# The last block of an encoder step: squares moved to ScalarE, whole-pass weight buffers, one table load, output pieces in free weight tiles on two store queues

## The chip, the cores and the metric

One core of one Trainium2 chip runs the whole program. Its engines are TensorE (PE; its weight loads are listed as PEld), VectorE (DVE), ScalarE (ACT), GpSimd (POOL) and SyncE (SP), which issues transfers. The metric is the device time of one execution in microseconds, the median over several runs. Lower is better.

## The reference, cut to what matters

The program computes one layer of a streaming encoder for 512 prompt frames, 16 meta tokens and 64 sample frames in float32: attention, then a feed-forward network, then a final RMSNorm. Only the end matters here:

```python
x = x + (jax.nn.silu(h @ lp['ffn_w_gate']) * (h @ lp['ffn_w_up'])) @ lp['ffn_w_down']
...
y_prompt = rmsnorm(xp[:, N_META:], final_norm_g)
y_sample = rmsnorm(xs, final_norm_g)

def rmsnorm(x, g):
    y = xf * lax.rsqrt(jnp.mean(xf * xf, axis=-1, keepdims=True) + EPS)
    return y * g
```

D_MODEL is 2048 and D_FF 5632. 576 tokens go through the feed-forward network (512 prompt and 64 sample tokens).

## The kernel before

**Layout.** Activations are kept transposed: a chunk of 128 model features lies on the partitions, the 576 tokens along the free dimension, in two halves `h` of 288 (`QH`). There are 16 such chunks, `y[0]` to `y[15]`. Float32 products are made of three products in a rounded format: `split(hi, lo, src)` rounds a tile to `hi` on ScalarE (L156) and takes the remainder `lo = src - hi` on VectorE (L153). `mm3` (L185 to L189) then adds `hi*hi`, `hi*lo` and `lo*hi` on TensorE.

**The down projection.** The 44 chunks of the hidden dimension come as 22 pairs and are taken in six blocks of 4, 4, 4, 4, 4 and 2 pairs. In the first five blocks `down_rows` uses a seven-product scheme (L1207 and L1211). The last block, of two pairs, uses plain products: `plain_rows`, called for each token half `h` (0, then 1) and each of eight pairs `d` of output chunks. One such call is called a pass here. It has 24 matmuls: two output chunks `f`, four weight chunks `k`, three products. For each `f`, it splits a 128x512 piece of weights into a `wh` and a `wl` tile, of which there are two buffers each. The raw weights of a pass (512 KB) come from HBM through two buffers of the tile `raw` in the pool `fd`; `fetch_raw` issues the load of a later pass on SyncE's queue behind each pass.

**The end of a pass.** VectorE adds the product to `y` (L1462). `squares` then squares the chunk half on GpSimd (L1485, L1488), adds the square to a running sum `sqs[h]` (L1489), and ScalarE multiplies the chunk in place by the gain of the final norm (L1490). ScalarE's scaling overwrites what GpSimd squares, so it waits for it.

**The output.** `finish(h, ahead)` is a generator. It turns `ahead` groups first: a group is four 128x128 transposes on TensorE into one bank of PSUM (L1503), for a set of four chunks `q` and a token group `j` (three token groups in each half, of 64, 128 and 96 or 128, 128 and 32 tokens). Then it sums the squares over the partitions with a matmul against ones for each token group (L1515, L1517), and takes the reciprocal root with a logarithm and an exponential on ScalarE and three small steps on VectorE (`rsqrt`, L165 to L169). Then, for each of twelve groups, it scales the turned rows by that root into an output piece `ot` of up to 128x512 (odd pieces on ScalarE, L1526, even ones on VectorE, L1528) and stores the piece from SyncE's queue (L140). The pieces lie in two buffers of a tag `ws` and one of a tag `ot`. The first half's `finish` is run in between the second half's passes, two steps behind each pass from the second on. The second half's runs behind the last pass.

**The order.** Tiles, buffers and semaphores are placed by a scheduler that simulates the program; within this part of the kernel it may issue an engine's instructions in another order than they are written, when their data allows. ScalarE's function tables are loaded by an instruction of its own (ACT_TABLE_LOAD), which the compiler puts ahead of a function that is not in the loaded set. The program preloads a set with logarithm and exponential once, at L134. The gate's Silu (L1364) loads another.

Of the kernel before, what the change touches and what calls it, by code (L numbers as in the profile page):

```python
# [11 lines left out]
F32 = mybir.dt.float32  # L12
F32R = mybir.dt.float32r
AF = mybir.ActivationFunctionType
ALU = mybir.AluOpType
# [4 lines left out]
P = 128  # L20
D = 2048
KC = D // P
SEQ, NM, NS, PAST = 512, 16, 64, 128
# [5 lines left out]
QH = TQ // 2  # L29
# [86 lines left out]
def encoder_step(  # L116
# [8 lines left out]
    V, S, G = nc.vector, nc.scalar, nc.gpsimd  # L125
    st = Streams()
    PE = OrderedTensorEngine(tc, st)
# [11 lines left out]
    def store(dst, src):  # L139
        nc.sync.dma_start(dst, src)  # L140
# [8 lines left out]
    def f32(ap):  # L149
        return ap.bitcast(F32)  # L150

    def sub_lo(lo, src, hi):
        V.tensor_tensor(lo, src, f32(hi), op=ALU.subtract)  # L153

    def split(hi, lo, src):
        S.activation(hi, src, AF.Copy)  # L156
        sub_lo(lo, src, hi)
# [27 lines left out]
    def mm3(outs, wh, wl, xh, xl, start, stop):  # L185
        n = len(outs)
        for p, (w, x) in enumerate(((wh, xh), (wh, xl), (wl, xh))):
            for i in range(n):
                PE.matmul(outs[i], w, x[i], start=start and p == 0, stop=stop and p == 2)  # L189
# [117 lines left out]
    with ExitStack() as ph:  # L307
# [29 lines left out]
        ones = f32(ones_r)  # L337
# [5 lines left out]
        with tc.tile_pool(name="xn", bufs=1, reuse_waits="tile") as xn:  # L343
# [41 lines left out]
            raw, both = {}, {}  # L385
# [702 lines left out]
    PE = nc.tensor  # L1088
    wp_cm.__exit__(None, None, None)
    def pool(name, side="left"):  # L1090
        cm = tc.tile_pool(name=name, bufs=1, side=side, reuse_waits="tile")
        return cm.__enter__(), lambda: cm.__exit__(None, None, None)
# [133 lines left out]
    ws = {}  # L1226
# [13 lines left out]
    for i in range(KC):  # L1240
# [3 lines left out]
        for hf in range(2):  # L1244
            wh, wl = ws.pop(2 * i + hf)
# [24 lines left out]
    fw, close_fw = pool("fw")  # L1270

    def load_pair(pool, src, c0, first=0):
        r = pool.tile([P, 16, 256], F32, name="raw", tag="raw", bufs=1)
        for i in range(2 - first):
            r0 = (first + i) * 1024
            load(r[:, 8 * i:8 * i + 8], src[r0:r0 + 1024, c0:c0 + 256].rearrange("(k p) c -> p k c", p=P))
        return r

    raw = load_pair(fr, w_gate, 0, 1)
# [8 lines left out]
    def squad(dtype=F32):  # L1288
        return fr.tile([P, 4, QH], dtype, name="s", tag="s", bufs=1)
# [37 lines left out]
    def builder(m0, count, plain, by_product=False):  # L1327

        places = {1: 0, 2: 1, 4: 2, 5: 3} if plain else {1: 0, 2: 2, 3: 3, 5: 4, 6: 5, 4: 6, 7: 7}
        todo = [(m, p) for m in range(m0, m0 + count) for p in places]  # L1330
        if by_product:
            order = [p for p, _ in CHAIN]
            todo.sort(key=lambda mp: order.index(mp[1]))
        for m, p in todo:
            hl = bc.tile([P, 2, QH], F32R, name=f"b{p}_{m % 8}")
            load(f32(hl), opspill[m, :, places[p]])
            operands[m % 8, p] = hl[:, 0], hl[:, 1]
            yield
# [47 lines left out]
    start = builder(0, blocks[0], False, True)  # L1386
    for u in range(FC // 2):
        out = {}
        for which, wsrc in (("g", w_gate), ("u", w_up)):
            first = turn == 0  # L1390
            now = raw[:, 0:8] if first else raw
            if turn < FC - 1:
                raw = load_pair((fr, fb)[(turn + 1) % 2], (w_up, w_gate)[turn % 2], (turn + 1) // 2 * 256)
            turn += 1
            c = fc.tile([P, 2, TQ], F32, name="c", tag="c" + which, bufs=1 + (which == "g"))
            chain = () if first else CHAIN if u == FC // 2 - 1 and which == "u" else WIDE
            take = combined(*quarters(c[:, 0, :], c[:, 1, :]), chain)
            if u == FC // 2 - 1 and which == "u":
                raw = fr.tile([P, 16, 256], F32, name="raw", tag="raw", bufs=1)
# [25 lines left out]
        g, w = out["g"], out["u"]  # L1425
# [4 lines left out]
        parts = [(0, w.rearrange("p f (h c) -> p (f h) c", h=2))]  # L1430
        if u < FC // 2 - blocks[-1]:
            b11, b12, b21, b22 = quarters(w[:, 0, :], w[:, 1, :])
            t = g.rearrange("p f (h c) -> p (f h) c", h=2)
# [9 lines left out]
    fd, close_fd = pool("fd")  # L1443

    def plain_rows(m0, n, d, hs, slots, done):

        banks = {(f, h): pmt()[:, 0:QH] for f in range(2) for h in hs}
        r = fetched.pop((m0, d, hs))
        for g in range(0, n, 2):
            for f in range(2):  # L1450
                wh = fw.tile([P, 4, P], F32R, name="wh", tag="wh", bufs=2)
                wl = fw.tile([P, 4, P], F32R, name="wl", tag="wl", bufs=2)
                split(wh, wl, r[:, 2 * g:2 * g + 4, f * P:(f + 1) * P])
                for k in range(4):
                    m = slots[g + k // 2]
                    ops = [operands[m, ((1, 2), (4, 5))[k % 2][h]] for h in hs]
                    mm3([banks[f, h] for h in hs], wh[:, k, :], wl[:, k, :], [o[0] for o in ops],
                        [o[1] for o in ops], g + k == 0, g + k == n + 1)
        for f in range(2):
            for h in hs:  # L1460
                c = y[2 * d + f][:, h * QH:(h + 1) * QH]
                V.tensor_tensor(c, c, banks[f, h], op=ALU.add)  # L1462
                done(2 * d + f, h)
# [12 lines left out]

    tok = [[(0, NS), (NS, P), (192, 96)], [(QH, P), (416, P), (544, 32)]]
    sqs = {}
    s4 = squad()

    def squares(i, h):
        c = y[i][:, h * QH:(h + 1) * QH]
        if i == 0:
            sqs[h] = s4[:, h]
            G.tensor_tensor(sqs[h], c, c, op=ALU.mult)  # L1485
        else:
            t = s4[:, 2 + i % 2]
            G.tensor_tensor(t, c, c, op=ALU.mult)  # L1488
            G.tensor_tensor(sqs[h], sqs[h], t, op=ALU.add)  # L1489
        S.activation(c, c, AF.Copy, scale=gE[:, i:i + 1])  # L1490

    def finish(h, ahead):

        groups = [(q, j) for q in range(4) for j in range(3)]

        def turned(q, j):
            o, n = tok[h][j]  # L1500
            ps = pmt()
            for k in range(4):
                PE.transpose(ps[0:n, k * P:(k + 1) * P], y[q * 4 + k][:, o:o + n], ident)  # L1503
            return ps

        held = []
        for g in groups[:ahead]:
            held.append(turned(*g))
            yield
        pc = pmt()  # L1510
        vc = yy.tile([P, 3], F32, name=f"vc{h}")
        rc = yy.tile([P, 3], F32, name=f"rc{h}")
        V.memset(vc, 1.0)
        for j, (o, n) in enumerate(tok[h]):
            PE.matmul(pc[0:n, 2 * j:2 * j + 2], sqs[h][:, o - h * QH:o - h * QH + n], ones[:, 0:2],  # L1515
                      start=True, stop=True)
            V.tensor_scalar(vc[0:n, j:j + 1], pc[0:n, 2 * j:2 * j + 1], 1.0 / D, EPS, op0=ALU.mult, op1=ALU.add)  # L1517
        rsqrt(rc, vc)
        yield
        for i, (q, j) in enumerate(groups):  # L1520
            o, n = tok[h][j]
            ps = held.pop(0) if held else turned(q, j)
            tag, bufs = ("ws", 2) if i % 3 < 2 else ("ot", 1)
            ot = yy.tile([P, 4, P], F32, name="ot", tag=tag, bufs=bufs).rearrange("p a b -> p (a b)")
            if i % 2:
                S.activation(ot[0:n], ps[0:n, :], AF.Copy, scale=rc[0:n, j:j + 1])  # L1526
            else:
                V.tensor_scalar(ot[0:n], ps[0:n, :], rc[0:n, j:j + 1], None, op0=ALU.mult)  # L1528
            cs = slice(q * 512, (q + 1) * 512)
            if o == 0:  # L1530
                store(y_sample[:, cs], ot[0:NS])
            else:
                store(y_prompt[o - NS:o - NS + n, cs], ot[0:n])
            yield

    wanted, m0 = [], 0
# [16 lines left out]
    for bi, n in enumerate(blocks):  # L1553
        slots = [(first + k) % 8 for k in range(n)]
        if bi + 1 < len(blocks):
            build = builder(first + n, blocks[bi + 1], bi + 2 == len(blocks))

            def step():
                next(spilling, None)
                if bi or d:  # L1560
                    next(build, None)

            for d in range(KC // 2):
                if bi == 0 and d + 1 < KC // 2:
                    load_y(d + 1)
                down_rows(first, n, d, slots, step)
                fetch_raw()
                if bi + d == 0:
                    for _ in spilling:
                        pass  # L1570
                    close_rw()
                    yy, close_yy = pool("yy", "right")
            for _ in build:
                pass
        else:
            before = iter(())
            for h in range(2):
                for d in range(KC // 2):
                    plain_rows(first, n, d, (h,), slots, squares)
                    fetch_raw()  # L1580
                    if d:
                        for _ in range(2):
                            next(before, None)
                before = finish(h, 5 * h)
            for _ in before:
                pass
        first += n
# [74 lines left out]
```

## Time and profile before

| | us |
|---|---|
| median of 3 runs | 2474.02 (2471.19 to 2477.39) |
| the profiled execution | 2474.84 |
| its span, first to last instruction | 2473.1 |
| first matmul of the last block (L189) | at 2386.85 |
| last block's passes end, transposes follow | at 2452.67 |
| first output piece of the second half | at 2459.27 |
| last store issued | at 2470.2 |

| engine | busy us | share of the span |
|---|---|---|
| PE | 2391.3 | 97% |
| DVE | 1856.6 | 75% |
| ACT | 1133.8 | 46% |
| POOL | 817.1 | 33% |

Times in the trace count from the span's first instruction. A row of the timeline has its start, its length in us, the engine, the line, the operation, the tiles as out<-in, and the count of instructions merged in it. In brackets stands the idle time of the engine before it and what ended that. In the rows of waits the numbers are the total in us, the times and the longest. In the rows of groups, busy time in us, mean ns of one, and then the idle time before them with its releasers. In the rows of transfers, KB each and the median us from issue to landing.

### The profile page before, as it was taken

How to read it: one execution, taken by the hardware profiler on the slowest of the kernel's cores; microseconds unless marked ns; L12 is line 12 of the kernel's file. 1: busy time of each engine (PE TensorE's matmuls, PEld its weight loads, DVE VectorE, ACT ScalarE, POOL GpSimd, SP SyncE). 2: the span in 40 equal slices, each digit the busy share in tenths (PEclk: the TensorE clock that was granted, in tenths of full speed). 3: DMA queues.
4: the chain of work that ended last, by engine and by line, in shares of the span. 5: the costliest groups of instructions: out<-in, count | busy, mean ns of one | idle time of the engine just before them, and what ended most of it. 6: DMA issues, size and time to landing. Idle time of an engine off the chain costs nothing. (4 is left out here: it accounts for less than half of the span.)

```text
span 2473.1 us, 44094 instructions
## 1 busy us (share of the span) xinstructions
PE 2391.3 (97%) x17544; PEld 2343.1 (95%) x17544; DVE 1856.6 (75%) x2748; ACT 1133.8 (46%) x1977; POOL 817.1 (33%) x525
## 2 busy tenths in 40 slices
PE   7999999999999999999999999999999999999997
PEld 7999999999998998999999999999999999999986
DVE  5666676666664788778778788787787888888875
ACT  5445545334453554444444444444444333333345
POOL 1100000120000455555555655555554222222245
PEclk9999999999999999999999999999999999999999
DMA  7432233253323644344444444443546873563334
GB/s 223 142 96 83 83 98 94 66 156 102 99 82 118 185 152 146 113 163 151 134 152 141 142 151 134 157 158 113 170 151 212 301 243 125 198 220 108 102 103 145
DMA packets 361972, 353.03 MB, mean 143 GB/s; under 512 B 25087, under 2 KB 319637, under 8 KB 361765
## 3 DMA queue, kind: packets, MB, share of 16 engines
q1 hardware_dynamic: 359535, 343.43, 43.5%
q0 software_dynamic: 1904, 6.24, 0.8%
q8 instruction: 138, 2.26, 0.4%
q10 hardware_dynamic: 325, 0.53, 0.1%
q14 instruction: 70, 0.57, 0.1%
HBM read 271.68 MB, written 81.16 MB: 143 GB/s over the span
## 5 line engine op out<-in xcount | busy, mean ns | idle before, releaser
L1207 PE MATMUL m<-b,wh 128*128 128x288 f32 x7168 | 1050.1, 295 | 16.6 <-DVE y L1472 8.5
L1207 PEld LDWEIGHTS m<-b,wh 128*128 128x128 f32 x7168 | 982.8, 188 | 23.6 <-issue 16.7
L153 DVE TENSOR_TENSOR wl<-raw,wh 128x512 fp32r<-128x512 f32 (+1 forms) x457 | 600.3, 1314 | 59.3 <-ACT wh L156 59.0
L1211 PE MATMUL m<-b,wl 128*128 128x288 f32 x3584 | 583.4, 298 | 11.7 <-DVE wl L153 11.5
L156 ACT ACTIVATE wh<-raw 128x512 fp32r<-128x512 f32 (+1 forms) x457 | 380.1, 832 | 410.3 <-PE m L1207 275.1
L1211 PEld LDWEIGHTS m<-b,wl 128*128 128x128 f32 x3584 | 512.4, 188 | 21.5 <-DVE wl L153 21.5
L1186 POOL TENSOR_TENSOR ws<-raw 128x1024 f32<-128x1024 f32 (+1 forms) x85 | 201.7, 2373 | 619.3 <-DVE wl L153 289.7
L156 ACT ACTIVATE wh<-ws 128x512 fp32r<-128x512 f32 (+1 forms) x170 | 144.2, 848 | 222.3 <-DVE ws L1189 180.0
L108 PE MATMUL ps<-xh,wh 128*128 128x296 f32 x992 | 225.9, 309 | 0.1
L108 PE MATMUL ps<-xl,wh 128*128 128x296 f32 x992 | 217.7, 301 | 0.3 <-DVE xl L161 0.3
L108 PE MATMUL ps<-xh,wl 128*128 128x296 f32 x992 | 216.9, 300 | 0.0
L1195 POOL TENSOR_TENSOR raw<-raw 128x1024 f32<-128x1024 f32 (+1 forms) x85 | 207.1, 2437 | 6.6
L153 DVE TENSOR_TENSOR wl<-ws,wh 128x512 fp32r<-128x512 f32 (+1 forms) x170 | 164.5, 968 | 17.5 <-ACT wh L156 17.4
L1346 DVE TENSOR_TENSOR c<-c,s 128x288 fp32r<-128x288 f32 x168 | 84.6, 533 | 110.6 <-POOL c L1437 59.7
L108 PEld LDWEIGHTS ps<-xh,wh 128*128 128x128 f32 x992 | 161.6, 191 | 3.7 <-issue 0.6
L108 PEld LDWEIGHTS ps<-xl,wh 128*128 128x128 f32 x992 | 162.3, 190 | 1.0 <-DVE xl L161 0.9
L108 PEld LDWEIGHTS ps<-xh,wl 128*128 128x128 f32 x992 | 162.2, 190 | 0.0
L1472 DVE TENSOR_TENSOR y<-y,m 128x288 f32<-128x288 f32 x280 | 126.0, 450 | 46.1 <-PE m L1211 46.1
L153 DVE TENSOR_TENSOR wl<-wr,wh 128x1024 fp32r<-128x1024 f32 (+1 forms) x110 | 120.7, 1097 | 31.7 <-ACT wh L156 30.4
L156 ACT ACTIVATE wh<-wr 128x1024 fp32r<-128x1024 f32 (+1 forms) x110 | 102.2, 929 | 75.3 <-PE ps L108 50.7
L1345 ACT ACTIVATE s<-c 128x288 fp32r<-128x288 f32 x168 | 63.2, 434 | 151.9 <-POOL c L1429 130.6
L1429 POOL TENSOR_TENSOR c<-c 128x576 f32<-128x576 f32 x44 | 101.1, 2297 | 80.6 <-DVE c L1303 78.9
(370 smaller groups left out, 3194.7 us busy)
## 6 DMA issues: line engine op xcount, KB each, us to landing
raw<-in_ffn_w_gate SPq DMA_DIRECT2D x44, 1024.0 KB, 5.5
raw<-in_ffn_w_up SPq DMA_DIRECT2D x44, 1024.0 KB, 7.9
b<-opspill SPq DMA_DIRECT2D x148, 288.0 KB, 5.9
raw<-in_ffn_w_down SPq DMA_DIRECT2D x38, 1024.0 KB, 5.6
wr<-in_w_in SPq DMA_DIRECT2D x56, 512.0 KB, 4.1
opspill<-s SPq DMA_DIRECT2D x42, 576.0 KB, 3.1
opspill<-c SPq DMA_DIRECT2D x42, 576.0 KB, 3.1
wr<-in_w_out SPq DMA_DIRECT2D x16, 512.0 KB, 4.3
```

Of the source, the lines that this page charges most:

```text
L108: self.tc.keep_in_program_order(self.pe.matmul(out, lhsT, rhs, start=start, stop=stop))
L153: V.tensor_tensor(lo, src, f32(hi), op=ALU.subtract)
L156: S.activation(hi, src, AF.Copy)
L1186: G.tensor_tensor(x, y, z, op=ALU.add)
L1195: G.tensor_tensor(y, x, y, op=ALU.subtract)
L1207: PE.matmul(banks[p], wh[:, k, :], x, start=first and new and k == 0 and x is hi, stop=False, skip_group_check=not new)
L1211: PE.matmul(banks[p], wl[:, k, :], hi, start=False, stop=last and k == n - 1, skip_group_check=not new)
L1345: S.activation(hi[:, k], src[:, k], AF.Copy)
L1346: V.tensor_tensor(src[:, k].bitcast(F32R), src[:, k], f32(hi[:, k]), op=ALU.subtract)
L1429: G.tensor_tensor(w[:, f, :], w[:, f, :], g[:, f, :], op=ALU.mult)
L1472: V.tensor_tensor(c, c, banks[p], op=ALU.add)
```

## The change

It has four parts, all in the last block and behind it.

1. `plain_rows`: the tiles `wh` and `wl` hold both output chunks of a pass (twice the size, still two buffers each), so weights can be split up to two passes ahead.
2. `squares`: in the first half the odd chunks are squared by ScalarE in place of GpSimd. In the second half the last two chunks (`LATE = 2`) are squared by ScalarE and not added to the running sum; the matmul against ones takes three parts, the sum and these two squares.
3. A preload of the set with logarithm and exponential, in front of the last block, pinned behind what ScalarE has before it. The first half's `finish` gets one step behind the second pass in place of two.
4. `finish`: in the second half eight of the twelve pieces lie in two tiles of the weights' tag `raw`, four pieces in each. The other four, and all pieces of the first half, lie in the two buffers of `ws`. The pieces 1, 3, 4 and 7 of the second half are stored from GpSimd's queue.

```diff
@@ plain_rows
         for g in range(0, n, 2):
+            wh = fw.tile([P, 2, 4, P], F32R, name="wh", tag="wh", bufs=2)
+            wl = fw.tile([P, 2, 4, P], F32R, name="wl", tag="wl", bufs=2)
             for f in range(2):
-                wh = fw.tile([P, 4, P], F32R, name="wh", tag="wh", bufs=2)
-                wl = fw.tile([P, 4, P], F32R, name="wl", tag="wl", bufs=2)
-                split(wh, wl, r[:, 2 * g:2 * g + 4, f * P:(f + 1) * P])
+                split(wh[:, f], wl[:, f], r[:, 2 * g:2 * g + 4, f * P:(f + 1) * P])
...
-                    mm3([banks[f, h] for h in hs], wh[:, k, :], wl[:, k, :], [o[0] for o in ops],
+                    mm3([banks[f, h] for h in hs], wh[:, f, k], wl[:, f, k], [o[0] for o in ops],
@@ squares
+    LATE = 2
...
-        if i == 0:
+        if h and i >= KC - LATE:
+            sqs[h, i] = s4[:, 2 + i % 2]
+            S.activation(sqs[h, i], c, AF.Square)
+        elif i == 0:
             sqs[h] = s4[:, h]
             G.tensor_tensor(sqs[h], c, c, op=ALU.mult)
         else:
             t = s4[:, 2 + i % 2]
-            G.tensor_tensor(t, c, c, op=ALU.mult)
+            if h or i % 2 == 0:
+                G.tensor_tensor(t, c, c, op=ALU.mult)
+            else:
+                S.activation(t, c, AF.Square)
             G.tensor_tensor(sqs[h], sqs[h], t, op=ALU.add)
@@ finish
-            PE.matmul(pc[0:n, 2 * j:2 * j + 2], sqs[h][:, o - h * QH:o - h * QH + n], ones[:, 0:2],
-                      start=True, stop=True)
+            parts = [sqs[h]] + [sqs[h, i] for i in range(KC - LATE, KC) if h]
+            for q in parts:
+                PE.matmul(pc[0:n, 2 * j:2 * j + 2], q[:, o - h * QH:o - h * QH + n], ones[:, 0:2],
+                          start=q is parts[0], stop=q is parts[-1])
...
-            tag, bufs = ("ws", 2) if i % 3 < 2 else ("ot", 1)
-            ot = yy.tile([P, 4, P], F32, name="ot", tag=tag, bufs=bufs).rearrange("p a b -> p (a b)")
+            k = i - i // 3
+            if h and i % 3 < 2:
+                if k % 4 == 0:
+                    four = fd.tile([P, 4, 512], F32, name="ot", tag="raw", bufs=2)
+                ot = four[:, k % 4]
+            else:
+                ot = yy.tile([P, 4, P], F32, name="ot", tag="ws", bufs=2).rearrange("p a b -> p (a b)")
...
+            out_queue = G.dma_start if h and i in (1, 3, 4, 7) else store
@@ the last block's loop
             before = iter(())
+            tc.keep_in_program_order(S.preload_act_table_set("natural_log_exp_and_others"))
             for h in range(2):
                 for d in range(KC // 2):
                     plain_rows(first, n, d, (h,), slots, squares)
                     fetch_raw()
-                    if d:
-                        for _ in range(2):
-                            next(before, None)
+                    for _ in range(min(d, 2)):
+                        next(before, None)
                 before = finish(h, 5 * h)
```

More of the change, by code (lines that the diff above doesn't have):

```diff
@@ L1529, in finish @@
             cs = slice(q * 512, (q + 1) * 512)
+            out_queue = G.dma_start if h and i in (1, 3, 4, 7) else store
             if o == 0:
-                store(y_sample[:, cs], ot[0:NS])
+                out_queue(y_sample[:, cs], ot[0:NS])
             else:
-                store(y_prompt[o - NS:o - NS + n, cs], ot[0:n])
+                out_queue(y_prompt[o - NS:o - NS + n, cs], ot[0:n])
             yield
```

## The prediction, made before the change was run

> **What bounds the kernel now.** I read the page first for the whole, then the chain of work that ended last, then the last block alone: its waits, its timeline engine by engine, and its groups by form.
>
> ```profile
> span 2473.1 us, 44094 instructions
> PE 2391.3 (97%) x17544; PEld 2343.1 (95%) x17544; DVE 1856.6 (75%) x2748; ACT 1133.8 (46%) x1977; POOL 817.1 (33%) x525
> ...
> by line: DMA out<-ot 6.9%; ACT ot L1526 1.5%; DVE ot L1528 1.5%; issue 1.2%; SPq L140 0.8%; DVE rc L169 0.2%; DVE vc L167 0.2%; DVE vc L168 0.2%; ACTq L1526 0.0%; DVEq L1528 0.0%
> ```
>
> TensorE (PE) is busy 97% of the span, so nearly everything that can be won lies where it idles. The second row is the chain within the window from 2385 to 2473 us: it is made of output pieces, and of their landing above all. So the change, which touches only the last block of rows (from 2386.85 us, the first matmul of L189) and the tail, has two stretches to work on: 66 us of passes, and a tail without matmuls.
>
> The passes. One pass is 24 matmuls for two row chunks of one token half. These rows are one pass in the middle of the first half, first TensorE, then the three engines that feed it.
>
> ```profile
> 2414.15 0.42 PE L189 MATMUL m<-b,wh 128*128 128x288 f32 x2
> ...
> 2416.92 0.43 PE L189 MATMUL m<-b,wh 128*128 128x288 f32 x2
> 2417.76 0.40 PE L189 MATMUL m<-b,wl 128*128 128x288 f32 x1 [0.41 <-DVE wl L153]
> ...
> 2414.48 1.16 POOL L1488 TENSOR_TENSOR s<-y 128x288 f32<-128x288 f32 x1
> ...
> 2418.33 1.17 POOL L1488 TENSOR_TENSOR s<-y 128x288 f32<-128x288 f32 x1
> ...
> 2415.68 0.54 ACT L1490 ACTIVATE y<-y,gT 128x288 f32<-128x288 f32 x1 [1.28 <-POOL s L1488]
> 2416.12 0.62 ACT L156 ACTIVATE wh<-raw 128x512 fp32r<-128x512 f32 x1
> ...
> 2416.77 0.93 DVE L153 TENSOR_TENSOR wl<-raw,wh 128x512 fp32r<-128x512 f32 x1 [0.78 <-ACT wh L156]
> ```
>
> Read it as a chain. GpSimd (POOL) squares a row chunk until 2415.64; the scaling on ScalarE (ACT) waits 1.28 us for that; the weight split of the next half pass stands behind the scaling in ScalarE's order, VectorE (DVE) takes its remainder from 2416.77 to 2417.70, and TensorE goes on at 2417.76 after an idle time. Between 2414.15 and 2416.92 lie seven triples of matmuls, 2.77/7 = 0.396 us each, so a pass of eight triples is worth 3.17 us; the pitch from one pass to the next is 2418.33 - 2414.48 = 3.85 us. About 0.68 us of each pass is lost. GpSimd sets that pitch:
>
> ```profile
> L1489 POOL TENSOR_TENSOR s<-s 128x288 f32<-128x288 f32 x30 | 28.3, 942 | 2.3
> L1488 POOL TENSOR_TENSOR s<-y 128x288 f32<-128x288 f32 x30 | 25.7, 855 | 8.9 <-DVE y L1462 8.7
> ...
> L156 ACT ACTIVATE wh<-raw 128x512 fp32r<-128x512 f32 x31 | 19.1, 619 | 4.6 <-PE m L189 2.3 <-DMA raw<-in_ffn_w_down 1.3 <-DVE wl L153 1.0
> L1490 ACT ACTIVATE y<-y,gT 128x288 f32<-128x288 f32 x32 | 17.1, 535 | 23.3 <-POOL s L1488 22.0 <-POOL s L1485 1.1
> ...
> L153 DVE TENSOR_TENSOR wl<-raw,wh 128x512 fp32r<-128x512 f32 x32 | 26.4, 827 | 11.7 <-ACT wh L156 11.4
> L1462 DVE TENSOR_TENSOR y<-y,m 128x288 f32<-128x288 f32 x32 | 14.4, 449 | 8.7 <-PE m L189 8.7
> ```
>
> Two squares and two adds are 2 x 0.855 + 2 x 0.942 = 3.59 us by the means, more than the 3.17 us that TensorE needs. What all this costs TensorE between 2386.5 and 2452.7 us, the waits of its weight loads say:
>
> ```profile
> PEld m L189 <- DVE wl L153: 5.6, 10, 0.7
> PEld m L189 <- ACT wh L156: 2.5, 3, 1.7
> ```
>
> Together 8.1 us: the whole stock that the passes can give.
>
> **The change part by part.**
>
> *Squares and split buffers.* In the first half (h = 0) the odd chunks' squares go to ScalarE. GpSimd is left with 0.855 + 2 x 0.942 = 2.74 us per pass, ScalarE has 2 x 0.619 + 2 x 0.535 and one square more, which I put at 0.535 (the scaling of the same shape on the same engine): 2.84 us. VectorE keeps 2 x 0.827 + 2 x 0.449 = 2.55 us. All three are now below 3.17. In the second half GpSimd keeps both squares (3.59 us) until the last two chunks, but there TensorE also turns two groups of four blocks per pass, which takes about 0.9 us more (24 records in 2.62 us, rows further down), so it needs 4.05 us and GpSimd fits. The other half of this part is that one weight buffer now holds both half passes, with two buffers as before: a split has a whole pass of 3.17 us from buffer free to first use, and split plus remainder is 0.62 + 0.93 us. A scaling that waits 1.28 us ahead of it no longer reaches TensorE. The load behind it moves forward with the split, so its lead stays. Bounds: 8.1 us if every wait goes, about 3.5 if only half do (scalings and splits still share ScalarE's order). I take 7.0, near the upper end, because all sums are under TensorE's; what I leave is one late load and the first pass.
>
> *Table loads.* Four loads become one.
>
> ```profile
> 2430.18 1.28 ACT L166 ACT_TABLE_LOAD   x1
> ...
> 2431.58 0.61 ACT L156 ACTIVATE wh<-raw 128x512 fp32r<-128x512 f32 x1
> ...
> 2432.24 0.92 PE L189 MATMUL m<-b,wh 128*128 128x288 f32 x3 [1.45 <-ACT wh L156]
> ```
>
> Two of them lie in the passes: here a split stands behind the load and TensorE waits; this is the 1.7 us wait counted in the 8.1 already. The third is hidden before the last logarithm; the fourth, before the last exponential, is on the chain and goes: 1.28 us. The new load sits on ScalarE ahead of the first pass. It delays a split there once, at the worst by its own 1.28 us, and the idle time of about one microsecond ahead of each split hides most of it; I cost it at nothing.
>
> The Trainium skill (ScalarE: Activation LUTs, What ACT_TABLE_LOAD costs) adds a drain of about 1.38 us to each load of 1283 ns, 2.66 us in all; by that the saving on the chain would be 2.7 and the time 1.4 us lower. The trace disagrees: the load from 2430.18 ends at 2431.46 and the exponential runs from 2431.47, so nothing stands between.
>
> *The norm of the second half.* The rows between the last matmul and the first output piece:
>
> ```profile
> 2452.67 2.78 PE L1503 MATMUL m<-ident,y 128*96 128x128 f32 x24
> ...
> 2454.15 0.80 POOL L1489 TENSOR_TENSOR s<-s 128x288 f32<-128x288 f32 x1
> ...
> 2455.29 0.28 PE L1515 MATMUL m<-ones,s 128*128 128x2 f32 x2
> ...
> 2456.74 0.15 DVE L1517 TENSOR_SCALAR vc<-m 32x1 f32<-32x1 f32 x1 [0.34 <-PE m L1515]
> ...
> 2457.15 1.28 ACT L166 ACT_TABLE_LOAD   x1
> ...
> 2459.27 1.40 DVE L1528 TENSOR_SCALAR ot<-m,rc 128x512 f32<-128x512 f32 x2
> ```
>
> GpSimd's last add ends at 2454.95, but TensorE is turning 24 blocks until 2455.29 anyway. So the last squares, moved past GpSimd, gain nothing here: their cover is these transposes. They cost something: each of the three token groups needs three matmuls against ones instead of one, six more. One takes two records, 0.28 us. The upper end is 6 x 0.28 = 1.7 us, the lower 0 (issued between the transposes); the steps alternate with VectorE on one bank, which speaks for the upper end, the 32-token group is shorter: +1.2. The first half's norm is now asked for one piece at a time (one step in the second pass instead of two), which moves one group of four transposes from before the last matmul to after it: 4 x 2.62/24 = 0.44 us from one side to the other, nothing in sum. Its output pieces share two buffers instead of three; two pieces per pass of 4.05 us against 0.75 evacuation and 2.2 landing, covered; without that cover 0.4 us for each of five passes.
>
> *The tail.* From 2459.27 to the end, 13.8 us. The rows of that stretch, of the output tile and of DMA:
>
> ```profile
> L140 SPq DMA_DIRECT2D out<-ot x12: 332/332/411, 2460.0 to 2470.2; - x12
> ...
>   DMA out<-ot: 12.4, 9
> ...
> DMA to landing us min/median/max: 1.9/2.1/2.4
> ...
> GB/s 0 0 0 0 160 380 380 410 297 83 0 0 101 386 273 303 386 255 6 0 0 303 380 143 392 362 131 0 0 137 386 238 65 410 333 143 0 0 0 0
> DMA packets 1344, 2.36 MB, mean 171 GB/s; under 512 B 192, under 2 KB 192, under 8 KB 1344
> ```
>
> Twelve pieces share three buffers, so nine of them wait for a landing, 12.4 us over both engines, and the DMA engines run in bursts with holes. After the change eight pieces have places of their own; only pieces 8 and 11 wait, for pieces 2 and 5. Evacuation: 0.70 us each on two engines (1.40 for two in the row above), 4.2 us for six. Piece 2 leaves VectorE at +1.4 and lands at about +3.6, pieces 8 and 10 follow to +5.0, piece 11 similarly on ScalarE; the last store would land near +7.5. The transfers are a second limit: 2.36 MB at the 380 GB/s of the full slices are 6.2 us, and the first bytes move in the fifth slice of 0.345 us, 1.4 us after the start: +7.6. With a few holes I take +8.2, and 0.9 us behind the last landing (2470.2 + 2.1 to 2473.1, as now): 9.1 in place of 13.8, a gain of 4.7. Bounds: 5.3 with no hole; below, the second queue:
>
> ```profile
> raw<-in_ffn_w_down POOLq DMA_DIRECT2D x2, 1024.0 KB, 7.2
> ...
> cos<-c_cos POOLq DMA_DIRECT2D x1, 296.0 KB, 6.4
> ```
>
> GpSimd issues four of the pieces (1, 3, 4, 7). Its transfers took 6.4 and 7.2 us to land. Piece 7 leaves ScalarE at about +2.8; with 7.2 it lands at +10.0, the end is +10.9 and the gain 2.9. I stay at 4.7, since those transfers stood behind others of their queue and were larger.
>
> The Trainium skill (SBUF — State Buffer) says that GpSimd cannot write the descriptors of its transfers while VectorE holds the shared port, which would strengthen that lower end. No run here shows a GpSimd store beside an evacuation yet.
>
> **Sum:** -7.0 (passes) - 1.3 (table load) + 1.2 (six matmuls) - 4.7 (tail) = -11.8 us against the profiled execution's own 2474.84: 2463.0. That execution stands 0.8 above the median of the runs, 2474.02, so I say 2462.2. A measurement of this kernel tells about 0.3%, 7.4 us, from no change.
>
> **Rivals.**
> 1. *The passes gain only half.* ScalarE's order binds: scalings still wait for GpSimd and splits behind them. For it: 22.0 us of waits of L1490 on L1488. Against: the whole-pass buffer. -3.5 - 1.3 + 1.2 - 4.7 = -8.3: about 2466.
> 2. *GpSimd's queue ends last.* Tail 2.9 instead of 4.7: -10.0, 2464; together with 1, -6.5 and 2468.
> 3. *Slower: the two halves of one weight buffer wait for each other.* If the tile is guarded as a whole, the second split of a pass starts only when the first half's matmuls are done. Then every pass bears a split, 0.62 us, and most of a remainder, 0.93, in TensorE's idle time: about 1.4 x 16 = 22.4 in place of 8.1, so +14.3 - 1.3 + 1.2 - 4.7 = +9.5, 2484. It turns slower by over 7.4 us once a pass loses over (8.1 + 4.8 + 7.4)/16 = 1.27 us. Against it speaks that two engines already write halves of one tile together:
>
> ```profile
> 2397.71 0.45 DVE L1462 TENSOR_TENSOR y<-y,m 128x288 f32<-128x288 f32 x1 [0.40 <-PE m L189]
> ...
> 2397.87 0.54 ACT L1490 ACTIVATE y<-y,gT 128x288 f32<-128x288 f32 x1 [1.28 <-POOL s L1488]
> ```
>
> These are chunks 5 and 4 of the third pass, two halves of one tile, and they overlap by 0.29 us.
>
> 4. *It does not do what it says:* the compiler's order puts the splits no earlier, and the passes stay at 3.85. Then only the tail and the load remain: -4.8, 2469.
>
> **Chances.** The forecast 0.62 (2459 to 2466, all faster). Rival 1: 0.12, half of it beyond 0.3%. Rival 2: 0.12, mostly faster, 0.03 of it (with rival 1) within. Rival 3: 0.06, slower. Rival 4: 0.08, within 0.3%. Faster 0.62 + 0.06 + 0.09 = 0.77, within 0.17, slower 0.06. The range runs from every wait and hole gone (-8.1 - 1.3 - 5.3 = -14.7, six matmuls hidden: 2459, and 1 us for the spread of the runs) to rival 4.
>
> **What will show it.** Pitch of the first-half passes near 3.2 us, and waits of L189's weight loads in that block near 1 us: the first step. One table load at L165, L166 and the preload together: the second. From the last matmul to the first output piece 6.6 + 0.4 + 1.2 - 1.3 = 6.9 us: the third. From there to the end 9.1 us, with DMA slices near 380 GB/s and no holes of a microsecond: the fourth. Wrong would make it: a pitch still at 3.85, or a last landing that belongs to a GpSimd store.

## The result, and the profile after

The changed kernel takes 2469.07 us (median of 16 runs, 2463.76 to 2473.97); the kernel before took 2474.24 beside it. The ratio is 0.9973, 95% interval 0.9964 to 0.9982: faster by 0.27%, some 6.7 us by the ratio and 5.2 by the medians. The forecast was 2462.2, so the direction held, the time lies at the upper edge of the range, and the gain is about half of the 11.8 us that were forecast (0.57 of them by the ratio, 0.44 by the medians).

The head of the page of the changed kernel, in one execution that took 2463.76 us:

```profile
span 2462.0 us, 44085 instructions
PE 2389.6 (97%) x17556; PEld 2342.0 (95%) x17556; DVE 1855.4 (75%) x2748; ACT 1131.7 (46%) x1984; POOL 809.0 (33%) x517
```

This execution is 11.1 us under the profiled one of before, but 4.6 us of that lie ahead of the change: the first matmul of L189 starts at 2382.34 here and at 2386.98 before (2386.85, which stands further up, is the start of its weight load). Over the profiles of this study that start lies anywhere between 2382.3 and 2395.8 us in code that no kernel alters. So single times are not compared below; the stretches of the last block are. Here they are in the changed kernel: passes, norm of the second half, tail (length, then busy time of PE, PEld, DVE, ACT, POOL, granted clock, DMA share and rate):

```profile
2382.34:2444.57 62.23, 59.05 (x434) 56.33 (x433) 42.23 (x74) 36.70 (x74) 40.44 (x50) 1.00 0.50 153
2444.57:2451.18 6.61, 6.23 (x59) 5.45 (x56) 2.15 (x8) 3.54 (x9) 0.56 (x1) 1.00 0.32 94
2451.18:2462.00 10.82, 1.92 (x16) 1.57 (x16) 4.11 (x6) 3.63 (x6) 2.23 (x4) 0.82 0.63 218
```

Before, they were 65.85, 6.44 and 13.83 us. The passes gained 3.6, the norm lost 0.2, the tail gained 3.0: 6.4 in all, which fits the ratio. Where the passes' other half went shows in the engines' timelines of the changed kernel (a stretch of the first half; ScalarE, VectorE, GpSimd):

```profile
2404.99 0.54 ACT L1497 ACTIVATE y<-y,gT 128x288 f32<-128x288 f32 x1 [1.23 <-POOL s L1493]
2405.44 1.14 ACT L156 ACTIVATE wh<-raw 128x512 fp32r<-128x512 f32 x2
...
2408.70 0.54 ACT L1497 ACTIVATE y<-y,gT 128x288 f32<-128x288 f32 x1 [1.23 <-POOL s L1493]
...
2406.08 1.29 DVE L153 TENSOR_TENSOR wl<-raw,wh 128x512 fp32r<-128x512 f32 x2 [1.69 <-ACT wh L156]
2407.30 0.81 DVE L1462 TENSOR_TENSOR y<-y,m 128x288 f32<-128x288 f32 x2
...
2407.05 1.00 POOL L1496 TENSOR_TENSOR s<-s 128x288 f32<-128x288 f32 x1 [1.20 <-ACT s L1495]
2408.01 0.66 POOL L1493 TENSOR_TENSOR s<-y 128x288 f32<-128x288 f32 x1
```

No engine is full, and yet the pitch is 2408.70 - 2404.99 = 3.71 us. The chain of releases that the profile follows back through this stretch says what makes it:

```profile
2405.44 1.14 ACT wh L156 x2
2406.57 0.34 ACT s L1495
...
2407.05 1.00 POOL s L1496
2408.05 0.64 POOL s L1493
...
2408.73 0.42 issue
2409.15 1.14 ACT wh L156 x2
```

It is a ring, a chain of waits that closes on itself. The two splits of a pass now come as a pair (2405.44 to 2406.58). ScalarE's own square of an odd chunk (L1495) stands behind the pair in its order. GpSimd's addition of that square (L1496) waits 1.20 us for it, and GpSimd's square of the next even chunk (L1493) stands behind the addition. ScalarE's scaling (L1497) waits 1.23 us for this square, and the next pair of splits stands behind the scaling. The legs are 1.14 + 0.34 + 1.00 + 0.64 + 0.42 us, with 0.17 us between them: 3.71. VectorE hangs beside the ring. Its two remainders wait 1.69 us for the pair and stand ahead of its two sums, but the first sum ends at 2407.74, before GpSimd's addition does at 2408.05.

And the waits of TensorE's weight loads in the passes:

```profile
PEld m L189 <- DVE wl L153: 2.7, 7, 0.4
PEld m L1524 <- DVE vc L1526: 2.5, 2, 1.6
PEld m L189 <- ACT wh L156: 0.3, 1, 0.3
```

Of the 8.1 us that L189 waited, 3.0 are left; but L1524, the first half's norm, waits 2.5 us where it waited 0.6. The tail, by its output tile, its transfers and its issues:

```profile
L140 SPq DMA_DIRECT2D out<-ot x8: 330/644/1407, 2452.0 to 2457.8; - x8
...
DMA to landing us min/median/max: 2.7/4.0/5.0
...
GB/s 15 0 0 0 0 53 357 372 190 303 281 243 296 410 311 281 273 288 349 440 357 425 402 387 364 372 402 379 319 319 159 144 220 46 0 0 0 0 0 0
...
out<-ot POOLq DMA_DIRECT2D x4, 256.0 KB, 4.0
```

The holes between bursts are gone. But SyncE's issues take a median of 0.64 and up to 1.41 us where they took 0.33, and pieces land after 4.0 us where they took 2.1.

### The profile page after: what moved, and what is told of

Same layout as the page of the kernel before. It is cut to its first block, busy times and chain, and to the rows that moved or that the text cites. A ratio compares the mean times of both kernels' runs of the same rounds, so it can differ in the third digit from the quotient of the medians.

```text
span 2462.0 us, 44085 instructions
## 1 busy us (share of the span) xinstructions
PE 2389.6 (97%) x17556; PEld 2342.0 (95%) x17556; DVE 1855.4 (75%) x2748; ACT 1131.7 (46%) x1984; POOL 809.0 (33%) x517
## 4 chain that ended last, share of the span: by engine, by line
PE 70%; DVE 12%; POOL 7%; ACT 4%; issue 3%; DMA 1%; DVEq 0%; ACTq 0%; POOLq 0%
PE m L1207 30%; PE m L1211 17%; PE ps L108 16%; POOL c L1429 4%; DVE wl L153 3%; PE m L189 2%; PE sp L108 2%; PE po L108 2%; PE tp L112 1%; ACT wh L156 1%; DVE c L1303 1%; DVE b L1110 1%; DVE c L1346 1%; POOL c L1434 1%; POOL c L1435 1%
## 5 line engine op out<-in xcount | busy, mean ns | idle before, releaser
L1211 PE MATMUL m<-b,wl 128*128 128x288 f32 x3584 | 583.7, 298 | 11.2 <-DVE wl L153 11.1
```

What stands on the lines that cost most here:

```text
L1211: PE.matmul(banks[p], wl[:, k, :], hi, start=False, stop=last and k == n - 1, skip_group_check=not new)
```

## Experiments

Eleven kernels, each an edit of the changed one (the last a combination). All stretches in us, from one profile each; "clock" says for how many us TensorE's granted clock stood at 0.50 behind the matmuls of the first half's norm, within the second half. Of the edited kernels only e4 and e11 have a ratio whose interval lies clear of the changed kernel's, so the edits are judged by the stretches that they touch.

| kernel | first half | second half | norm | tail | sum | clock | ratio to before (95%) |
|---|---|---|---|---|---|---|---|
| before | 29.9 | 35.9 | 6.4 | 13.8 | 86.1 | - | 1 |
| changed | 27.5 | 34.7 | 6.6 | 10.8 | 79.6 | - | 0.9973 (0.9964 to 0.9982) |
| e1_sp_only | 27.3 | 36.3 | 6.6 | 10.1 | 80.3 | 3.4 | 0.9982 (0.9970 to 0.9994) |
| e2_no_tail | 27.9 | 37.7 | 6.6 | 13.9 | 86.2 | 6.8 | 0.9990 (0.9976 to 1.0004) |
| e3_half_buffers | 28.8 | 35.5 | 6.6 | 10.8 | 81.8 | - | 0.9977 (0.9963 to 0.9992) |
| e4_pool_squares | 31.1 | 38.4 | 6.6 | 10.7 | 86.8 | 6.8 | 0.9998 (0.9984 to 1.0012) |
| e5_act_squares | 26.8 | 33.0 | 6.6 | 10.7 | 77.1 | - | 0.9958 (0.9942 to 0.9974) |
| e6_no_preload | 27.8 | 34.7 | 8.6 | 10.8 | 81.9 | - | 0.9977 (0.9961 to 0.9994) |
| e7_late0 | 27.8 | 36.3 | 5.6 | 10.7 | 80.4 | 3.4 | 0.9967 (0.9953 to 0.9981) |
| e8_act_queue | 26.9 | 36.3 | 6.6 | 11.1 | 80.9 | 3.4 | 0.9975 (0.9963 to 0.9986) |
| e9_mm_first | 27.2 | 32.9 | 6.3 | 11.0 | 77.5 | - | 0.9965 (0.9953 to 0.9978) |
| e10_all_places | 27.1 | 34.7 | 6.6 | 10.2 | 78.6 | - | 0.9977 (0.9966 to 0.9987) |
| e11_best | 26.3 | 31.0 | 5.0 | 10.3 | 72.6 | - | 0.9937 (0.9924 to 0.9951) |

### The passes: e5, e4, e3

My theory was a ring through GpSimd's squares, with VectorE's sums as a leg of it; the rival, that ScalarE and VectorE close one alone.

```diff
# e5_act_squares: all squares on ScalarE
-            G.tensor_tensor(sqs[h], c, c, op=ALU.mult)
+            S.activation(sqs[h], c, AF.Square)
...
-            if h or i % 2 == 0:
-                G.tensor_tensor(t, c, c, op=ALU.mult)
-            else:
-                S.activation(t, c, AF.Square)
+            S.activation(t, c, AF.Square)
```

> The changed kernel with every square, of both halves, on ScalarE; GpSimd only adds. My theory of the first half's pitch of 3.71 us is a loop: ScalarE's scaling waits for GpSimd's square, the splits stand behind the scaling, VectorE's sums stand behind the splits' remainders, and the next square waits for the sum. With GpSimd out of it the pitch falls to 3.2 to 3.3 us and the stretch from the first matmul of L189 to the last from 62.2 to 58 to 59.5 us, the time by about 3. The rival is that the loop is closed by ScalarE and VectorE alone, by their order, or that ScalarE fills up: the pitch stays at 3.6 to 3.8 and the stretch at 61.5 or more.

The pitch behind the lead fell to 3.31 to 3.34 us and the passes to 59.8, a little over the 3.3 and the 59.5 that I expected at most. ScalarE's timeline shows why (its waits in the first half, then one row of a pass):

```profile
ACT wh L156 <- DMA raw<-in_ffn_w_down: 4.9, 3, 2.3
ACT s L1492 <- DVE y L1462: 1.8, 5, 0.4
...
2414.64 0.44 ACT L1492 ACTIVATE s<-y 128x288 f32<-128x288 f32 x1 [0.36 <-DVE y L1462]
```

No wait of ScalarE for GpSimd is left; the ring now runs over ScalarE and VectorE alone (split, two remainders, sum, square, scaling), with 0.36 us of waiting. So the theory holds in that GpSimd's squares closed the ring (0.4 of the 0.54 us that a pass lost), and the rival for the rest. The leg through VectorE's sums that I had in mind for the changed kernel is not what held it there: by the chain above, it was ScalarE's square and GpSimd's addition. Only 0.7 us of the 2.4 that the passes gained lie in the first half, since the ring's pitch sets in late there. The rest lies in the second half's first three passes, up to the one with the norm: 3.31, 3.63 and 6.45 us, where the changed kernel's took 3.72, 4.00 and 7.40.

```diff
# e4_pool_squares: the first half's odd squares back on GpSimd
-            if h or i % 2 == 0:
-                G.tensor_tensor(t, c, c, op=ALU.mult)
-            else:
-                S.activation(t, c, AF.Square)
+            G.tensor_tensor(t, c, c, op=ALU.mult)

# e3_half_buffers: weight buffers of half a pass
             for f in range(2):
-                split(wh[:, f], wl[:, f], r[:, 2 * g:2 * g + 4, f * P:(f + 1) * P])
+                wh = fw.tile([P, 4, P], F32R, name="wh", tag="wh", bufs=2)
+                wl = fw.tile([P, 4, P], F32R, name="wl", tag="wl", bufs=2)
+                split(wh, wl, r[:, 2 * g:2 * g + 4, f * P:(f + 1) * P])
```

> The changed kernel with the first half's odd squares back on GpSimd. GpSimd then needs 3.6 to 3.8 us per pass and a pitch of 3.8 to 3.85 is expected in the first half, against 3.71 now: the stretch of L189 grows by 0.8 to 1.2 us. If GpSimd's load was never what set the pitch, nothing changes, within 0.3; if moving these squares to ScalarE is the main gain, it grows by 3 or more.

> The changed kernel with weight buffers of half a pass, as before the change. If the whole-pass buffer carries the gain of the passes, the stretch of L189 goes from 62.2 us to 64.5 or more. If the squares on ScalarE carry it, 62 to 63. If the larger buffer lets the splits crowd ahead of VectorE's sums and so closes the loop of 3.71 us per pass, it falls below 62.

Without the ScalarE squares (e4) the passes take 69.5 us, 7.3 more, far over the 0.8 to 1.2 that I expected. Not all of that is the edit's. In this profile the granted clock stood at 0.50 for 6.83 us, of which TensorE was busy for 5.65, so I estimate that about 2.8 us are the clock's. That leaves 4.5 us, and 0.8 over the kernel before. The first half, in which the clock was 1.00 in every profile, is the safer measure. It took 29.9 us before, 31.1 with whole-pass buffers and GpSimd's squares (e4), 28.8 with half-pass buffers and ScalarE's squares (e3), and 27.5 with both edits. In e4 the pitch is 4.38, not the 3.85 of before (ScalarE, VectorE, GpSimd):

```profile
2414.52 0.54 ACT L1494 ACTIVATE y<-y,gT 128x288 f32<-128x288 f32 x1 [2.33 <-POOL s L1492]
2414.96 1.14 ACT L156 ACTIVATE wh<-raw 128x512 fp32r<-128x512 f32 x2
...
2415.61 2.14 DVE L153 TENSOR_TENSOR wl<-raw,wh 128x512 fp32r<-128x512 f32 x2 [1.51 <-ACT wh L156]
2417.68 0.81 DVE L1462 TENSOR_TENSOR y<-y,m 128x288 f32<-128x288 f32 x2
...
2418.20 0.67 POOL L1492 TENSOR_TENSOR s<-y 128x288 f32<-128x288 f32 x1 [0.99 <-DVE y L1462]
...
PEld m L189 <- DVE wl L153: 5.2, 8, 0.7
PEld m L189 <- ACT wh L156: 2.8, 6, 0.5
PEld m L1521 <- DVE vc L1523: 2.4, 2, 1.5
```

Here VectorE is on the ring: the two remainders of a pair (2.14 us, where they took 1.29 in the changed kernel) stand ahead of its sums, GpSimd's square waits for a sum, the scaling for the square, and the next pair for the scaling. The waits of L189's weight loads are 8.0 us again. So in the first half the larger buffer alone is a loss of 1.2 us and the ScalarE squares alone a gain of 1.1, and together they gain 2.4. With half-pass buffers (e3) the pitch was 3.41 us in three of the first half's passes, shorter than the 3.71 with whole-pass buffers. But the loss began with the second pass, while the larger buffer's lead kept three of the changed kernel's first five passes at 3.17 us and the other two at 3.43 and 3.40. All passes of e3 together took 64.3 us, 1.5 less than before and 2.1 more than the changed kernel, just under the 64.5 from which I would have said that the buffer carries the gain.

### The first half's norm: e9

```diff
# e9_mm_first: all matmuls against ones, then VectorE's reads
         for j, (o, n) in enumerate(tok[h]):
             ...
                 PE.matmul(pc[0:n, 2 * j:2 * j + 2], ...)
+        for j, (o, n) in enumerate(tok[h]):
             V.tensor_scalar(vc[0:n, j:j + 1], pc[0:n, 2 * j:2 * j + 1], ...)
```

> The changed kernel with all matmuls against ones of a half issued before VectorE reads the first of them, so that the token groups no longer alternate between TensorE and VectorE on one bank. In the changed kernel TensorE stands still twice in the pass with the first half's norm (0.6 and 1.4 us, behind VectorE's splits), and in most profiles its granted clock then falls to 0.50 for 3 us. If that alternation is the cause, the second half's passes fall from 34.7 us (36.3 where the clock fell) to 31 to 33, with no 0.50 in the clock, and the stretch from the last matmul of L189 to the first evacuation from 6.6 to 5.5 to 6.0. If the norm's wait merely moves to the running sum of GpSimd, the second half stays above 34.

The second half took 32.9 us, 1.8 less, and the waits of the weight loads in the passes hold no norm any more. The row of the matmuls of the last norm, now one run of 18 records, stands below it:

```profile
PEld m L189 <- DVE wl L153: 3.1, 8, 0.4
...
2447.36 1.68 PE L1524 MATMUL m<-ones,s 128*128 128x2 f32 x18
```

The last norm itself gained only 0.3 us (6.6 to 6.3), less than I expected: nine matmuls in a row take 1.68 us before VectorE may start. What this alternation costs in other executions is shown by e1, whose second half is 1.6 us longer than the changed kernel's with the same code there. Its windows in that pass (TensorE's busy time is the first number behind the length, the granted clock the third from the end):

```profile
2428.00:2430.00 2.00, 1.03 (x6) 0.79 (x6) 0.56 (x3) 1.43 (x3) 1.92 (x3) 1.00 0.70 217
2430.00:2431.00 1.00, 0.29 (x3) 0.29 (x4) 1.00 (x3) 0.61 (x2) 0.92 (x2) 1.00 0.26 90
...
2432.00:2433.00 1.00, 1.00 (x6) 1.00 (x6) 0.83 (x2) 0.30 (x3) 0.67 (x1) 0.50 0.08 22
...
2434.00:2435.00 1.00, 1.00 (x8) 0.86 (x7) 0.45 (x1) 0.90 (x2) 0.12 (x1) 0.66 0.61 205
```

TensorE is idle for half of the first window and most of the second; then it is full, but at a clock of 0.50 for 3.41 us (2431.26 to 2434.67). The profiles of e7 and e8 have the same, those of e2 and e4 a clock of 0.50 for 6.83 us; the changed kernel, e6 and e10 have the idle time without it. The second halves of the five are 36.3 us and longer, the other three's 34.7.

### The second half's norm and the table load: e7, e6

```diff
# e7_late0
-    LATE = 2
+    LATE = 0
# e6_no_preload
-            tc.keep_in_program_order(S.preload_act_table_set("natural_log_exp_and_others"))
```

> The changed kernel with the last two squares back on GpSimd and in the running sum, so one matmul against ones for each token group in place of three. By my prediction GpSimd is hidden behind the transposes: from the last matmul of L189 to the first evacuation 6.6 us becomes 5.2 to 5.7. If the last squares on GpSimd are late, it becomes 6.6 or more.

> The changed kernel without the table load ahead of the last block, so that the logarithm and the exponential load a table each, in both halves. On the chain behind the last matmul 1.28 us come back: 6.6 becomes 7.9 us. In the passes the two loads of the first half's norm are either hidden by the whole-pass buffers (stretch of L189 at 62.2 within 0.5) or cost 1.3 to 2 as they did before.

With the last squares back on GpSimd the norm takes 5.6 us, 1.0 less. GpSimd, first matmul against ones and VectorE's first read in e7:

```profile
2461.21 0.80 POOL L1496 TENSOR_TENSOR s<-s 128x288 f32<-128x288 f32 x1
...
2462.78 0.28 PE L1524 MATMUL m<-ones,s 128*128 128x2 f32 x2
2463.10 0.16 DVE L1526 TENSOR_SCALAR vc<-m 128x1 f32<-128x1 f32 x1 [1.99 <-PE m L1524]
```

GpSimd is done at 2462.01, 0.7 us before its sum is read, so moving its last squares buys nothing and six matmuls cost 1.0. Without the preload the norm takes 8.6 us, 1.95 more (I had expected 7.9), and the passes only 0.3 more: there, the two loads of the first half's norm are nearly hidden by now. ScalarE in e6:

```profile
2456.51 0.68 ACT L1540 ACTIVATE ot<-m,rc 96x512 f32<-96x512 f32 x1 [1.27 <-DMA out<-ot]
...
2457.64 1.28 ACT L165 ACT_TABLE_LOAD   x1
2458.94 0.21 ACT L165 ACTIVATE rc<-vc 128x3 f32<-128x3 f32 x1
2459.16 1.28 ACT L166 ACT_TABLE_LOAD   x1
2460.45 0.21 ACT L166 ACTIVATE rc<-rc 128x3 f32<-128x3 f32 x1
```

Both loads are on the chain here. The first, hidden before the change, now stands behind the last output piece of the first half, and 0.7 us of it show. That piece waits 1.27 us for a landing, because these pieces have two buffers in place of three: in e2, where they have three again, ScalarE's row of it has no wait.

### The tail: e2, e1, e8, e10

```diff
# e2_no_tail: pieces in "ws" (2) and "ot" (1) as before, all stores from SyncE
# e1_sp_only, e8_act_queue
-            out_queue = G.dma_start if h and i in (1, 3, 4, 7) else store
+            out_queue = store                                                  # e1
+            out_queue = S.dma_start if h and i in (1, 3, 4, 7) else store      # e8
# e10_all_places: e1, and
+            elif h:
+                if i % 6 == 2:
+                    pair = fw.tile([P, 2, 4, P], F32R, name="ot", tag="wh", bufs=2)
+                ot = f32(pair[:, i // 3 % 2]).rearrange("p a b -> p (a b)")
```

> The changed kernel with the output pieces as before the change: two buffers of one tag and one of another, all stores from SyncE. If the parts simply add, the stretch from the first evacuation to the end is 13.8 us again (10.8 with the change) and the time lies 3.0 above the changed kernel, 2.5 to 3.5 below the kernel before. If pieces in weight tiles were worth less than that, because the waits only move, under 2.

> The changed kernel with all twelve pieces of the second half stored from SyncE's queue, none from GpSimd's. From the first evacuation to the end the changed kernel took 10.8 us. If GpSimd's transfers slow the queue beside them (its last four SyncE issues took 0.94 to 1.41 us instead of 0.33), this stretch falls to 9.3 to 9.8 us, 1.0 to 1.5 us less in all. If the second queue is indifferent, because the waits of pieces 8 and 11 for their buffers decide, it stays at 10.8 within 0.3. If it is a help, as the change has it, the stretch grows to 11.5 or more.

> The changed kernel with pieces 1, 3, 4 and 7 stored from ScalarE's queue in place of GpSimd's. If what costs is GpSimd's way of issuing, a second queue of the other kind gives 9.3 to 9.8 us from the first evacuation to the end, as with SyncE alone or 0.2 better. If any second queue costs, it stays at 10.8. If the four issues delay ScalarE's evacuations (4 x 0.35 us in its order), it gives 10.2 to 10.8.

> All stores from SyncE, and the four other pieces of the second half also in tiles of their own (the weight split's buffers, free by then), so that no piece waits for a landing. With SyncE alone and these waits the stretch from the first evacuation to the end took 10.1 us. If the transfers themselves are the limit (2.36 MB, about 6.2 us at full rate, and they ran without holes), it stays at 9.8 to 10.2. If the last pieces' waits still count, it falls to 9.0 to 9.5.

The tail is 13.9 without this part (e2), so the part is worth 3.0 to 3.1 us, as expected. That the sum of e2's stretches is no lower than before the change, where I had expected 2.5 to 3.5 less, goes with its 6.83 us at a clock of 0.50 (TensorE was busy for 6.31 of them, so some 3.2 us by my estimate). With SyncE alone (e1) the tail is 10.1, 0.7 less than with the second queue: less than the 1.0 that I expected, but the sign is clear. Seven profiles with GpSimd's queue beside SyncE's have tails of 10.7 to 11.0 us, the three with SyncE alone 10.1 to 10.3. The places made the gain, the second queue took 0.7 of it back. ScalarE as the second queue is no better, 11.1 (I had expected 9.3 to 10.8), so it is not GpSimd's way of issuing alone. SyncE alone, issues, landings and rates:

```profile
L140 SPq DMA_DIRECT2D out<-ot x12: 330/395/448, 2462.2 to 2467.8; - x12
...
DMA to landing us min/median/max: 2.4/2.8/3.2
...
GB/s 0 0 0 0 0 0 211 357 414 365 389 349 244 349 406 349 341 381 316 244 341 414 365 397 381 268 292 316 349 381 389 349 244 130 16 0 0 0 0 0
```

The transfers now run without a hole for some 7 us; that, and not the waits for places, is the limit. e10 agrees: with a place for every piece the tail stays at 10.2. With two queues the DMA engines are just as busy in the middle, but the row of the changed kernel ends with 159, 144 and 220 GB/s. SyncE's last four issues take 0.94 to 1.41 us there, one behind the other, and the last is done 7.98 us after the first piece, against 6.81 in e1. The wait for a place is not the reason: ScalarE waits 2.45 us for the buffer of its last piece in the changed kernel and 2.29 in e1, and scales that piece at 5.46 us in the changed kernel, sooner than at 5.70 in e1. Why an issue takes longer beside a second queue is not shown. With ScalarE's queue (e8) the place does count: the last piece waits 3.32 us and is scaled only at 7.77.

The Trainium skill (DMA: Bandwidth & Descriptors, Issuing engines are not separate DMA queues) has it that transfers of all issuing engines run on the same 16 DMA engines and interleave, and a second issuer saves issue time alone. The trace agrees in that two queues bring no more speed, 10.8 and 11.1 us against 10.1 with one; the saved issue time does not show, since SyncE's issues got longer.

### Put together: e11

```diff
# e11_best: e5, e9, LATE = 0 (e7), e1 and e10
```

> Put together: every square on ScalarE, all sums in GpSimd's running sum (one matmul against ones for each token group), these matmuls ahead of VectorE's reads, all stores from SyncE, every piece of the second half in a place of its own. If the parts add, the stretch of L189 takes 56.5 to 58.5 us (62.2 with the change, 65.9 before), then 4.5 to 5.2, then 9.3 to 10.1: 70.5 to 73.5 from the first matmul of the block to the end, 13 to 15 us under the kernel before, a ratio near 0.9945. If ScalarE, with 2.8 to 3.5 us per pass, takes the place of GpSimd as the bound of the second half, the stretch stays at 60 or more.

Its three stretches, and what is left of the waits of L189:

```profile
2383.98:2441.29 57.31, 57.12 (x434) 56.07 (x433) 38.88 (x74) 45.68 (x98) 26.34 (x28) 1.00 0.53 165
2441.29:2446.26 4.97, 4.97 (x47) 4.61 (x44) 1.97 (x9) 2.56 (x7) 1.60 (x2) 1.00 0.44 139
2446.26:2456.50 10.24, 1.92 (x16) 1.57 (x16) 4.03 (x6) 3.53 (x6) 0.00 (x0) 0.77 0.66 232
...
PEld m L189 <- DVE wl L153: 0.4, 1, 0.4
```

The parts add: 72.6 us, 13.5 under the kernel before and 7.1 under the change; the ratio 0.9937 (0.9924 to 0.9951) fits, 15.6 us (12 to 19). TensorE is busy in 57.12 of the 57.31 us of the passes, and in the norm without a gap.

## Why the prediction was half right

The direction held, and of the four terms the table load and the six matmuls came out near their price. The two large ones, passes and tail, were half and two thirds of what was forecast. The measured -6.4 us is what rivals 1 and 2 give together (-6.5 and 2468), though not all by their mechanisms. The time lies outside the 2459 to 2466 that had the chance of 0.62. Only the wider range, which reached up to the price of rival 4, took it in, and not because the forecast's own terms held; that much is luck.

1. *Passes, -7.0; measured -3.6.* The step that failed is "A scaling that waits 1.28 us ahead of it no longer reaches TensorE". I summed each engine's work per pass (2.84, 2.74 and 2.55 us, all under 3.17) and took the fullest engine for the pitch. The waits form a ring over ScalarE and GpSimd, and a ring costs the sum of its legs: 3.71 us. The first passes did run at 3.17 us, until the lead of the buffers was used up. Rival 1 named the mechanism (ScalarE's order) and its size (-3.5), with a chance of 0.12. But the ring is only half of what is missing: L189's weight loads still wait 3.0 us where I left 1.1. The other half is a term that I put at nothing, the first half's norm. Its matmuls waited 0.6 us before and 2.5 after, since VectorE's reads stand between splits that now come in pairs; e9 takes these waits away. Against these two, 0.4 us of the gain is the group of transposes that moved behind the passes.
2. *The larger buffer as a gain.* I took it for the half of the part that frees TensorE. With GpSimd's squares it costs 1.2 us in the first half (e4), with ScalarE's squares it gains 1.3 (28.8 to 27.5): it gives a lead and lengthens the ring.
3. *Table load, -1.3.* Right in kind. Within the kernel as changed the preload is worth 1.95 us on the chain (e6), since there the first load would show as well. It shows because the first half's output pieces share two buffers, which I had taken as covered.
4. *Norm, six matmuls, +1.2.* Measured 1.0 (e7). That the last squares moved past GpSimd gain nothing held, GpSimd is done 0.7 us early. The stretch in all: +0.4 + 1.2 - 1.3 forecast, +0.2 measured.
5. *Tail, -4.7; measured -3.0.* The transfers were the limit, as one of my two bounds had it, but mis-sized: I took 6.2 us for them from the fullest slices, they take about 7.1 even from one queue, and the end is some 1.4 us behind the last packet where I took 0.9 from the last landing. The remaining 0.7 is the second queue. The gain is that of rival 2 (2.9), but not by its mechanism: the GpSimd stores landed after 4.0 us, not 7.2, the last landing was SyncE's, and it was SyncE's issues that grew longer.
6. Rivals 3 and 4 fell. The two halves of a weight buffer are guarded apart: TensorE never waited a whole split per pass. And the splits did move ahead: the first five passes ran at 3.17 to 3.43 us, not at 3.85.

## What to carry to other kernels

When every engine's work fits into the period and the period is longer all the same, follow the waits around: engine by engine to the one that released it, until the chain closes on itself; the pitch is the sum of that ring. Here it shrank when GpSimd's squares were taken out of it (3.71 to 3.32), while the deeper buffer bought a lead of five passes and a longer ring behind them (3.41 to 3.71). Matmuls and reads that alternate on one bank are better issued as all matmuls first where the reading engine has other work in between (1.8 us in e9's second half, 0.3 in its last norm). A second store queue gave nothing where the transfers themselves filled the DMA engines, and it made the first queue's issues longer. And look at the granted clock of every profile before reading a stretch as an edit's price: in e4 it was some 2.8 of 7.3 us.

## What the runs showed of the hardware that was not expected

TensorE's granted clock fell to 0.50 around the first half's norm in five profiles (e1, e2, e4, e7, e8) and not in three with the same two idle times (the changed kernel, e6, e10: 0.6 and 1.4 us). Where it fell it stayed there for 3.41 us or for 6.83, twice that. The loss is about half of TensorE's busy time in it: 1.7 us in e1, beside 2.0 us of idle time. The Trainium skill (TensorE: Matmul & The Clock Gate, The HAM clock gate) gives half rate as the state after an idle window of about 3.4 us: the half agrees with the 0.50 measured, the idle time here was shorter and broken.

Within a profile the changes of the clock lie whole multiples of 3.41 us apart (e1: 2431.26, 2434.67, 2461.98, 2465.39). In the step of 3.41 us before the fall TensorE was busy for 1.58 us in e1, 1.82 in e2, 1.57 in e7 and 1.40 in e8. Counted in the same steps back from a later change, the idlest step around this norm had 2.0 us in the changed kernel, e6 and e10, and the clock held. But e4 fell behind a step with 2.35 us, so what decides is not settled.

A SyncE issue is not of fixed length: 0.33 us by the median in the tail before the change, 0.40 with SyncE alone and the transfers without a hole (e1), up to 1.41 with GpSimd's queue beside it and up to 1.01 with ScalarE's (e8).
